# An attention and mixture-of-experts layer on one core: 38 of the 64 experts run in pairs as plain fp32 in the two column halves of TensorE

## The chip, the cores and the metric

The kernel runs on one core of a Trainium2 chip. The metric is the device time of one execution in microseconds (us); the times before are three runs, and one further execution was recorded by the hardware profiler. A core has the engines TensorE (PE, with its weight loads shown apart as PEld), VectorE (DVE), ScalarE (ACT), GpSimd (POOL) and SyncE (SP, which here only issues transfers), and 16 DMA engines that move data between HBM and the core's memory. SBUF is the on-chip memory of 128 partitions, PSUM the accumulators that TensorE writes.

## The reference

One transformer layer on 512 tokens of 1024 numbers: two attention branches, a layer norm, and a mixture of experts with a second layer norm. The change touches the mixture of experts alone:

```python
scores = jax.nn.sigmoid((hf @ w_router).astype(jnp.float32))      # 512 tokens x 64 experts
...
_, top_idx = lax.top_k(jnp.where(emask, biased, -jnp.inf), TOP_K)  # 8 experts for each token
top_w = top_s / jnp.sum(top_s, -1, keepdims=True) * ROUTED_SCALE
...
def step(acc, inp):                                                # one expert e, its tokens t
    t, w, e = inp
    xb = x_pad[t]
    hb = jax.nn.silu(xb @ w1_e[e]) * (xb @ w3_e[e])                # 1024 -> 256
    return acc.at[t].add((hb @ w2_e[e]) * w[:, None]), None        # 256 -> 1024
...
shared = (jax.nn.silu(hf @ ws1) * (hf @ ws3)) @ ws2                # every token
return (routed + shared).reshape(b, s, d)                         # ffn
...
return layer_norm(ALPHA * h + ffn, ln2_g, ln2_b)
```

There are 512 x 8 = 4096 rows of work, 64 for a mean expert. Each expert has 3 MB of fp32 weights, 192 MB in all.

## The kernel before

The attention part runs until about 480 us and is left as it is but for one line of stores. What follows is the expert stage.

**Tiles.** A tile is a list of up to 128 token rows. `tiles` has 35 of them: the first four experts alone (fixed, so that work can start before the experts are sorted), two large experts alone, and 29 pairs of a large with a small expert. The experts were sorted by their number of tokens (`order`). In a pair the list holds the union of both experts' tokens, both experts are applied to all its rows, and each row has a weight for each expert, zero where it wasn't routed there. From the routing of the reference's own inputs the 35 lists hold 3905 rows.

**What one expert costs.** Its weights come as three loads of 1 MB (`expert_load`, L820, issued by SP: two for the first products, one for the last), each into one page of SBUF. There are 16 pages; 5 hold shared weights and the transposed tokens until the shared expert is done, then 5 are taken by tiles called `dum`, so that 9 or 10 are left for expert weights. ACT and DVE split each half page into a high and a low part (`split`, L196 and L197; `LOOK` = 2 pieces ahead), and every product is made of three matmuls in fp32r (`mm3`, L302 to L304). An expert has six steps of 12 half products: four steps of the first product (`p_` 0 to 3) and two of the last (`p_` 4 and 5, which run among the next expert's steps), 36 matmuls of 512 columns.

**Rows in and out.** For each tile POOL issues a gather, an indirect transfer that brings the listed rows (4 KB each) from `hD` in HBM into the tile's partitions, one row for each partition (`gather_rows`, L1178), and a scatter that adds the tile's results to the rows of `accD` in HBM (`finish`, L1219). Empty slots are out of bounds and move nothing. PE transposes the gathered rows (L1190).

**What accD holds.** At first ALPHA times the tokens (`ya` in `h_rows`, made by ACT and stored from its queue). The shared expert's four blocks are added by POOL's accumulating transfers (`shared_out`, L1250), whose work is strewn between the expert steps. After the last scatter `accD` is loaded in four blocks `z` and normalised (L1475 to L1491).

**Order.** The expert stage stands in a `manual_schedule`: every engine, DVE and SP included, executes in the order in which the loop over `steps` writes the instructions. A load waits on SP until its page is free, which for a page of weights is when DVE has split its second half.

Of the kernel before, what the change touches and what calls it, by code (L numbers as in the profile page):

```python
# [19 lines left out]
S, D = 512, 1024  # L20
NE = 64
N_STAT = 4
N_SOLO = 2
N_TILE = N_STAT + N_SOLO + (NE - N_STAT - N_SOLO) // 2
# [14 lines left out]
for _k, _w in (("cb", 128), ("dn", 256), ("dp", 256), ("ut", 128), ("inv", 8), ("tok", 8),  # L39
               ("ident", 128), ("iota1", 128), ("lt", 64), ("lte", 64), ("rq", 128), ("stat", 3)):  # L40
    _C[_k] = (_n, _n + _w)
    _n += _w
# [4 lines left out]
def const_pack():  # L47
# [20 lines left out]
    rq[N_STAT:N_STAT + N_SOLO] = np.arange(N_SOLO)  # L68
    npair = (64 - N_STAT - N_SOLO) // 2
    m = np.arange(npair)  # L70
    rq[N_STAT + N_SOLO::2] = N_SOLO + m
    rq[N_STAT + N_SOLO + 1::2] = N_SOLO + 2 * npair - 1 - m
# [6 lines left out]
    tok[:, :, 1] = 128.0 * np.arange(4)[None] - 512.0  # L79
# [51 lines left out]
def hybrid_layer_kernel(tc, xT, xn, pos, w_idx, w_blk, w_uk, w_uv, w_ab, w_o, w_r, w_s13, w_s2, w_e, ln, b_gate,  # L131
# [514 lines left out]
    aoT = [None, None]  # L646

# [175 lines left out]


# [105 lines left out]
    pos1 = cpool.tile([128, 4, N_TILE], F32, name="pos1")  # L930
    pos0 = cpool.tile([128, 4, N_STAT], F32, name="pos0")
    hD = dpool.tile([S, D], F32, name="hD")
    accD = dpool.tile([S, D], F32, name="accD")
# [81 lines left out]
    def h_rows(c):  # L1015
# [18 lines left out]
        ya = t4([D], name="ya")  # L1034
        if YG:
            G.tensor_scalar(ya, hz[c], ALPHA, None, op0=OP.mult)
        else:
            A.activation(ya, hz[c], AF.Copy, scale=ALPHA)
        nc.scalar.dma_start(accD[c * 128:(c + 1) * 128], ya)
# [14 lines left out]
    def one_hot(pos_, i):  # L1054
        oh = t2([4, 128], BF16, name="oh")
        V.tensor_tensor(oh, C("iota1").unsqueeze(1).broadcast_to([128, 4, 128]),
                        pos_[:, :, i].unsqueeze(2).broadcast_to([128, 4, 128]), op=OP.is_equal)
        return oh

    def slot_mm(oh, qs, tw_):  # L1060
# [5 lines left out]
        if tw_ is not None:  # L1066
            for c in range(4):
                mm(pl[:, 2:2 + 3 * len(qs)], lhsT=oh[:, c],
                   rhs=tw_[:, c, qs[0]:qs[0] + len(qs)].rearrange("p q a -> p (q a)"), start=(c == 0), stop=(c == 3))
        return pl  # L1070

    def slot_rows(pl):

        lo_ = small([1], "li", bufs=4)
        V.tensor_scalar(lo_, pl[:, 1:2], 512.0, None, op0=OP.add)
        ii = small([1], "ii", I32, bufs=8)
        V.tensor_tensor(ii, pl[:, 0:1], lo_, op=OP.add)
        return ii

    def slot_weights(pl, n):  # L1080
        wv = small([2], "wv", bufs=8)
        V.tensor_reduce(wv[:, :n], pl[:, 2:2 + 3 * n].rearrange("p (q a) -> p q a", a=3), axis=AX.X, op=OP.add)
        return wv

    def tile_list(oh, qs, tw_):
        pl = slot_mm(oh, qs, tw_)
        return [slot_rows(pl), slot_weights(pl, len(qs))]

    tiles = [[q] for q in range(N_STAT + N_SOLO)]
    tiles += [[q, q + 1] for q in range(N_STAT + N_SOLO, NE, 2)]  # L1090
# [7 lines left out]
    selt = cpool.tile([128, 4, N_TILE], BF16, name="selt")  # L1098

    def order():  # L1100
# [46 lines left out]

        q0 = N_STAT + N_SOLO
        V.tensor_copy(selt[:, :, :q0], selq[:, :, :q0])
        V.tensor_tensor(selt[:, :, q0:], selq[:, :, q0::2], selq[:, :, q0 + 1::2], op=OP.max)  # L1150
        yield
        places(pos1, selt, N_TILE)
# [4 lines left out]
    def spill():  # L1157
        q0 = N_STAT + N_SOLO
        pc = ps_o()
        for c in range(4):  # L1160
            mm(pc[0:1, 0:N_TILE], lhsT=ones_b[:, 0:1], rhs=selt[:, c], start=(c == 0), stop=(c == 3))
        nt = t2([3, N_TILE], name="nt")[0:1]
        for b in range(3):
            V.tensor_scalar(nt[:, b], pc[0:1, 0:N_TILE], 128.5 + 128.0 * b, None, op0=OP.is_gt)
        V.tensor_tensor(nt[:, 0], nt[:, 0], nt[:, 1], op=OP.add)
        V.tensor_tensor(nt[:, 0], nt[:, 0], nt[:, 2], op=OP.add)
        V.tensor_copy(nbi[:, 0:q0], nt[:, 0, 0:q0])
# [347 lines left out]
```

## Time and profile before

| what | value |
|---|---|
| median of three runs | 1146.54 us (1145.93 to 1146.61) |
| the profiled execution's own time | 1148.03 us |
| its span, first to last instruction | 1146.3 us |
| PE / DVE / ACT / POOL busy in the span | 94% / 77% / 61% / 20% |
| bytes moved by the DMA engines | 285.99 MB, mean 249 GB/s |
| mean granted clock of PE | 0.974 of 2.4 GHz |

Busy shares are averages over the span. The profile also lists who waited for whom, the chain of work that ended last, and the share of the 16 DMA engines that was busy in a stretch. That share sums the times of packets, which overlap a little, so it can pass 1. A plain fp32 matmul has two records in the trace, an fp32r one has one.

### The profile page before, as it was taken

How to read it: one execution, taken by the hardware profiler on the slowest of the kernel's cores; microseconds unless marked ns; L12 is line 12 of the kernel's file. 1: busy time of each engine (PE TensorE's matmuls, PEld its weight loads, DVE VectorE, ACT ScalarE, POOL GpSimd, SP SyncE). 2: the span in 40 equal slices, each digit the busy share in tenths (PEclk: the TensorE clock that was granted, in tenths of full speed). 3: DMA queues.
4: the chain of work that ended last, by engine and by line, in shares of the span. 5: the costliest groups of instructions: out<-in, count | busy, mean ns of one | idle time of the engine just before them, and what ended most of it. 6: DMA issues, size and time to landing. Idle time of an engine off the chain costs nothing.

```text
span 1146.3 us, 15930 instructions
## 1 busy us (share of the span) xinstructions
PE 1073.5 (94%) x5453; PEld 856.3 (75%) x5454; DVE 886.4 (77%) x1716; ACT 693.9 (61%) x1079; POOL 224.1 (20%) x138
## 2 busy tenths in 40 slices
PE   8999999999999997899999999999999999999970
PEld 7777988767778886477777888887878888777750
DVE  6588567863224976678878999999999999989966
ACT  5652454544532512157767888888888788777850
POOL 0323422121240003212211111111212111111110
PEclk9989999999999998899999999999999999999995
DMA  9322100203115563579999899999999999999943
GB/s 350 123 74 74 37 7 32 75 1 111 38 57 208 197 246 110 204 262 317 336 383 363 287 371 401 383 397 384 389 394 381 399 382 398 383 394 384 383 115 149
DMA packets 51157, 285.99 MB, mean 249 GB/s; under 512 B 8574, under 2 KB 8830, under 8 KB 22784
## 3 DMA queue, kind: packets, MB, share of 16 engines
q1 hardware_dynamic: 37392, 240.09, 53.3%
q0 software_dynamic: 11088, 37.24, 12.6%
q10 hardware_dynamic: 2592, 7.60, 1.9%
q8 instruction: 44, 0.72, 0.2%
q14 instruction: 41, 0.34, 0.1%
HBM read 262.86 MB, written 26.76 MB: 253 GB/s over the span
## 4 chain that ended last, share of the span: by engine, by line
PE 78%; DVE 12%; DMA 5%; ACT 3%; issue 2%; SPq 0%; ACTq 0%; POOLq 0%; DVEq 0%
PE pj L302 12%; PE pj L304 11%; PE pj L303 11%; PE ps_s L303 10%; PE ps_s L302 10%; PE ps_s L304 10%; DMA we<-in_w_e_dram 3%; PE ps_t L1190 3%; PE pj L1229 2%; DVE sp L197 1%; PE pj L1247 1%; PE ps_o L1207 1%; ACT aw L599 1%; DVE aw L669 1%; PE ps_o L678 1%
## 5 line engine op out<-in xcount | busy, mean ns | idle before, releaser
L197 DVE TENSOR_TENSOR sp<-we,sp 128x1024 fp32r<-128x1024 f32 x379 | 446.7, 1220 | 29.6 <-ACT sp L196 25.5
L196 ACT CAST sp<-we 128x1024 fp32r<-128x1024 f32 x384 | 381.8, 1051 | 12.5 <-DMA we<-in_w_e_dram 7.5
L302 PE MATMUL ps_s<-sp,xt 128*128 128x512 f32 x512 | 222.4, 434 | 0.0
L303 PE MATMUL ps_s<-sp,xt 128*128 128x512 f32 x512 | 203.7, 398 | 1.0 <-DVE sp L197 1.0
L304 PE MATMUL ps_s<-sp,xt 128*128 128x512 f32 x512 | 202.1, 395 | 0.0
L197 POOL TENSOR_TENSOR sp<-raw,sp 128x1024 fp32r<-128x1024 f32 x38 | 90.8, 2388 | 232.5 <-ACT sp L196 232.5
L1219 POOL DMA_INDIRECT accD<-y,ii x35 | 56.3, 1609 | 384.2 <-ACT si L1200 325.8
L303 PEld LDWEIGHTS ps_s<-sp,xt 128*128 128x128 f32 x512 | 96.7, 189 | 33.2 <-DVE sp L197 12.4
L302 PEld LDWEIGHTS ps_s<-sp,xt 128*128 128x128 f32 x512 | 96.5, 189 | 23.5 <-issue 4.3
L304 PEld LDWEIGHTS ps_s<-sp,xt 128*128 128x128 f32 x512 | 96.2, 188 | 20.4 <-issue 0.2
L302 PE MATMUL pj<-sp,at 128*128 128x512 f32 x256 | 100.6, 393 | 0.0
L304 PE MATMUL pj<-sp,at 128*128 128x512 f32 x256 | 100.1, 391 | 0.0
L303 PE MATMUL pj<-sp,at 128*128 128x512 f32 x256 | 99.7, 389 | 0.0
L302 PE MATMUL pj<-sp,xh 128*128 128x512 f32 (+1 forms) x224 | 94.5, 424 | 5.0 <-ACT sp L196 5.0
L303 PE MATMUL pj<-sp,xh 128*128 128x512 f32 (+1 forms) x224 | 87.2, 389 | 0.1
L304 PE MATMUL pj<-sp,xl 128*128 128x512 f32 (+1 forms) x224 | 86.9, 388 | 0.0
L1178 POOL DMA_INDIRECT xg<-hD,ii x35 | 49.3, 1407 | 139.3 <-PE ps_t L1190 119.6
L196 ACT CAST sp<-raw 128x1024 fp32r<-128x1024 f32 (+2 forms) x45 | 45.2, 1004 | 50.2 <-PE pj L304 38.1
L302 PEld LDWEIGHTS pj<-sp,xh 128*128 128x128 f32 x224 | 55.3, 248 | 12.4 <-ACT sp L196 4.7
L196 ACT CAST xt<-ps_t 128x512 fp32r<-128x512 f32 x70 | 41.1, 587 | 38.6 <-PE ps_t L1190 36.4
L1218 ACT COPY y<-pj 128x512 f32<-128x512 f32 x69 | 40.1, 587 | 33.8 <-PE pj L304 31.0
L303 PEld LDWEIGHTS pj<-sp,xh 128*128 128x128 f32 x224 | 56.0, 250 | 3.8 <-DVE sp L197 0.5
(365 smaller groups left out, 1833.6 us busy)
## 6 DMA issues: line engine op xcount, KB each, us to landing
we<-in_w_e_dram SPq DMA_DIRECT2D x189, 1024.0 KB
raw<-in_w_blk_dram SPq DMA_DIRECT2D x20, 1024.0 KB
raw<-in_w_o_dram SPq DMA_DIRECT2D x4, 1024.0 KB
rab<-in_w_ab_dram SPq DMA_DIRECT2D x4, 768.0 KB
s<-in_w_s_dram SPq DMA_DIRECT2D x3, 1024.0 KB
we<-in_w_e_dram POOLq DMA_DIRECT2D x3, 1024.0 KB, 11.2
xr<-in_xT_dram SPq DMA_DIRECT2D x8, 256.0 KB
hD<-h ACTq DMA_DIRECT2D x4, 512.0 KB
```

The source lines that it names most:

```text
L196: A.copy(hi, raw)
L197: (eng or V).tensor_tensor(lo, raw, hi, op=OP.subtract)
L302: mm(o_, lhsT=ah, rhs=bh, start=start, stop=False)
L303: mm(o_, lhsT=ah, rhs=bl, start=False, stop=False)
L304: mm(o_, lhsT=al, rhs=bh, start=False, stop=stop)
L599: A.activation(aw[:, hh, :n], aw[:, hh, :n], AF.Exp, scale=0.125, bias=nms[hh], accum_out=den[hh])
L669: V.tensor_scalar(L, L, rd, None, op0=OP.mult)
L1178: G.indirect_dma_start(out=xg, out_offset=None, in_=hD[:, :], in_offset=bass.IndirectOffsetOnAxis(ap=ii[:, 0:1], axis=0), bounds_check=S - ...
L1190: T.transpose(pt[:, k * 128:(k + 1) * 128], xg[:, kk_ * 128:(kk_ + 1) * 128], ident)
L1218: A.copy(y[:, n * 512:(n + 1) * 512], py[n])
L1219: G.indirect_dma_start(out=accD[:, :], out_offset=bass.IndirectOffsetOnAxis(ap=ii[:, 0:1], axis=0), in_=y, in_offset=None, compute_op=OP.a ...
L1229: mm(p_, lhsT=hT[c // 2][:, c % 2, kt], rhs=s13[kt // 4][:, kt % 4], start=(kt == 0), stop=(kt == 7))
```

## The change

- **Tiles.** 45 instead of 35: the four fixed experts and 22 more alone (the 22 largest of the sorted ones), and 19 pairs of the 38 smaller ones. Pairs and single experts alternate, three single ones stand last (`tile_plan`). By the reference's routing the largest expert in a pair has 64 tokens.
- **Pairs.** The first expert has slots 0 to 63, the second slots 64 to 127, each its own list (`one_hot`, `slot_mm`). The lists hold 4096 rows. The weights are used as they come, without `split`: one plain fp32 matmul for each half, with 64 stationary columns, into its own half of the PSUM partitions. `xt` and `at` of a pair are one fp32 copy. The page of a pair's weights becomes free when PE has used it, not when DVE has split it.
- **Sums.** `accD` has 1024 rows; the second expert of a pair adds to the upper 512 (`jj`), since a token may be in both halves of one transfer. Both halves are set to zero early: POOL clears a tile, ACT issues eight stores in the attention part. `ya` and its stores go. The shared expert's rows are stored to `shD` from ACT's queue instead of being added by POOL.
- **The end.** At the first step of the third tile from the end SP issues eight loads of `hD` and `shD` (4 MB) into the four `z` pages; at the first step of the last tile but one DVE adds them (L1469), and SP loads the upper half of `accD`; at the first step of the last tile DVE adds that (L1473). After the last scatter the lower half is loaded and added (L1521), then normalised as before.
- **Pages.** The `dum` tiles go, so 14 pages serve weights once the shared expert is done. Single experts keep three split pieces in hand (`HOLD`), taken past a pair.

```diff
+N_SOLO = 22
+N_PAIR = (NE - N_STAT - N_SOLO) // 2
+N_END = 3
+def tile_plan():
+    tiles, q, s = [[i] for i in range(N_STAT)], N_STAT, 0
+    for m in range(N_PAIR):
+        tiles.append([q, q + 1])
+        q += 2
+        while s * N_PAIR < (m + 1) * (N_SOLO - N_END):
+            tiles.append([q])
+            q, s = q + 1, s + 1
+    return tiles + [[q + j] for j in range(N_END)]
...
+    accD = dpool.tile([2 * S, D], F32, name="accD")
+    shD = dpool.tile([S, D], F32, name="shD")
...
+        zero = t4([D], name="zero")
+        G.memset(zero, 0.0)
+        for a_ in range(0, 2 * S, 128):
+            nc.scalar.dma_start(accD[a_:a_ + 128], zero)
...
-        ya = t4([D], name="ya")
...
-            A.activation(ya, hz[c], AF.Copy, scale=ALPHA)
-        nc.scalar.dma_start(accD[c * 128:(c + 1) * 128], ya)
...
-        G.dma_start(accD[c * 128:(c + 1) * 128], y, accum_op=OP.add)
+        nc.scalar.dma_start(shD[c * 128:(c + 1) * 128], y)
...
-            while len(pieces) <= LOOK and len(pieces) < len(steps) - n:
-                split_next()
-            hi, lo = pieces.pop((q, p_))
+            while len(pieces) < HOLD:
+                if not split_next():
+                    break
+            if not pair:
+                hi, lo = pieces.pop((qs[0], p_))
...
+                    if pair:
+                        for q, rs_ in zip(qs, HALF):
+                            w1_ = wts[q][k // 4].rearrange("p (k n) -> p k n", k=4)
+                            mm(phs[i][rs_], lhsT=xts[i][:, k, rs_], rhs=w1_[:, k % 4], start=(k == 0), stop=(k == 7))
...
+            if i == NTL - N_END and p_ == 0:
+                for c in range(4):
+                    zs.append(page([2, D], name="z"))
+                    nc.sync.dma_start(zs[c][:, 0], hD[c * 128:(c + 1) * 128])
+                    nc.sync.dma_start(zs[c][:, 1], shD[c * 128:(c + 1) * 128])
+            if i == NTL - 2 and p_ == 0:
+                for c in range(4):
+                    V.scalar_tensor_tensor(zs[c][:, 0], zs[c][:, 0], ALPHA, zs[c][:, 1], op0=OP.mult, op1=OP.add)
+                    nc.sync.dma_start(zs[c][:, 1], accD[S + c * 128:S + (c + 1) * 128])
+            if i == NTL - 1 and p_ == 0:
+                for c in range(4):
+                    V.tensor_tensor(zs[c][:, 0], zs[c][:, 0], zs[c][:, 1], op=OP.add)
```

DVE at the end of the expert stage, before the change: `sp` is the low part of a split piece of weights, `si` and `at` are an expert's activation and its transposed low part, `y` is a result copied out of PSUM.

```order
L1201 SCALAR_TENSOR_TENSOR si<-si,wv,ps_s 128x256
L197 TENSOR_TENSOR sp<-we,sp 128x1024 x2
L197 TENSOR_TENSOR at<-ps_o,at 128x256
L197 TENSOR_TENSOR sp<-we,sp 128x1024 x4
L1201 SCALAR_TENSOR_TENSOR si<-si,wv,ps_s 128x256
L197 TENSOR_TENSOR sp<-we,sp 128x1024 x2
L197 TENSOR_TENSOR at<-ps_o,at 128x256
L197 TENSOR_TENSOR sp<-we,sp 128x1024 x3
L1201 SCALAR_TENSOR_TENSOR si<-si,wv,ps_s 128x256
L197 TENSOR_TENSOR at<-ps_o,at 128x256
L197 TENSOR_TENSOR sp<-we,sp 128x1024
L1216 COPY y<-pj 128x512
```

The same engine near the end, after the change (L217 is the old L197, L1228 the old L1201; `xt` is a low part of transposed rows):

```order
L217 TENSOR_TENSOR sp<-we,sp 128x1024
L1469 SCALAR_TENSOR_TENSOR z<-z 128x1024 x4
L217 TENSOR_TENSOR sp<-we,sp 128x1024
L217 TENSOR_TENSOR at<-ps_o,at 128x256
L217 TENSOR_TENSOR xt<-ps_t,xt 128x512
L217 TENSOR_TENSOR sp<-we,sp 128x1024 x2
L217 TENSOR_TENSOR xt<-ps_t,xt 128x512
L217 TENSOR_TENSOR sp<-we,sp 128x1024 x2
L1228 SCALAR_TENSOR_TENSOR si<-si,wv,ps_s 128x256
L217 TENSOR_TENSOR sp<-we,sp 128x1024
L1473 TENSOR_TENSOR z<-z 128x1024 x4
L217 TENSOR_TENSOR sp<-we,sp 128x1024
```

Four additions that read loaded `z` tiles (L1469) now stand on DVE ahead of the last eleven splits (four more follow the rows shown), and four more (L1473) ahead of the last five.

SP at the end of the expert stage, after the change, from the last expert's last load on (L841 is the old L820). Before it, the last load of weights was followed by nothing until the stage was over.

```order
L841 DMA we<-in_w_e_dram 128x2048
L1465 DMA z<-hD 128x1024
L1466 DMA z<-shD 128x1024
L1465 DMA z<-hD 128x1024
L1466 DMA z<-shD 128x1024
L1465 DMA z<-hD 128x1024
L1466 DMA z<-shD 128x1024
L1465 DMA z<-hD 128x1024
L1466 DMA z<-shD 128x1024
L1470 DMA z<-accD 128x1024 x4
```

The eight loads of `z` are issued behind the last load of weights, on the same queue.

## Rows read from the trace of the kernel before

**Rows 1.** Stretches of the expert stage: us, busy time by engine, clock, DMA share, GB/s

```profile
700.00:750.00 50.00, 50.00 (x254) 40.14 (x252) 47.92 (x62) 40.45 (x55) 7.67 (x5) 1.00 1.02 387
...
1000.00:1050.00 50.00, 49.24 (x249) 38.73 (x248) 45.94 (x61) 39.44 (x53) 7.48 (x5) 1.00 1.02 395
```

**Rows 2.** Waits, 700 to 1080 us: ACT's, then SP's queue

```profile
ACT sp L196 <- DMA we<-in_w_e_dram: 7.5, 6, 2.4
...
SPq L820 <- DVE sp L197: 275.8, 106, 4.5
```

**Rows 3.** The chain that ended last, 985 to 1147 us: start, length, what

```profile
1002.17 20.18 DMA we<-in_w_e_dram
...
1040.19 19.42 DMA we<-in_w_e_dram
```

**Rows 4.** Line L820, the weight loads: issues from 1002.1 to 1040.1 us; after 493 us

```profile
L820 SPq DMA_DIRECT2D we<-in_w_e_dram x12: 332/333/338, 1002.2 to 1035.5; - x12
...
L820 SPq DMA_DIRECT2D we<-in_w_e_dram x180: 332/333/722, 493.3 to 1080.7; - x180
```

**Rows 5.** Two stretches with one kind of transfer: weights alone; the first gather alone

```profile
394.00:400.00 6.00, 6.00 (x29) 4.95 (x28) 6.00 (x10) 2.06 (x5) 0.00 (x0) 1.00 1.00 421
...
481.20:482.20 1.00, 1.00 (x9) 0.29 (x8) 0.00 (x0) 0.00 (x0) 1.00 (x2) 0.50 0.53 86
```

**Rows 6.** Gathers after 495 us; gathers 700 to 1090 us; all scatters

```profile
L1178 POOL DMA_INDIRECT xg<-hD,ii x32: 1015/1500/1819, 497.2 to 1050.4; - x32
...
L1178 POOL DMA_INDIRECT xg<-hD,ii x20: 1287/1501/1512, 700.9 to 1050.4; - x20
...
L1219 POOL DMA_INDIRECT accD<-y,ii x35: 1564/1581/2209, 512.9 to 1112.7; - x35
```

**Rows 7.** Chain: plain fp32 matmuls, full width and halves, fp32r matmul, transposes

```profile
266.21 1.02 PE ps_o L678 x16
...
458.89 6.87 PE pj L1229 x16
...
1083.12 0.44 PE ps_t L1190 x4
...
1107.02 0.23 PE pj L302
```

**Rows 8.** Groups on DVE by form, 700 to 1080 us: busy, mean ns, idle before

```profile
L197 DVE TENSOR_TENSOR sp<-we,sp 128x1024 fp32r<-128x1024 f32 x250 | 294.5, 1220 | 16.3 <-ACT sp L196 13.9
...
L197 DVE TENSOR_TENSOR xt<-ps_t,xt 128x512 fp32r<-128x512 f32 x41 | 28.0, 683 | 0.0
...
L1201 DVE SCALAR_TENSOR_TENSOR si<-si,wv,ps_s 128x256 f32<-128x256 f32 x41 | 19.6, 478 | 3.5 <-ACT si L1200 3.3
L197 DVE TENSOR_TENSOR at<-ps_o,at 128x256 fp32r<-128x256 f32 x41 | 17.1, 418 | 0.0
```

**Rows 9.** Chain from the end of PE's work on; then a DVE group after 1111 us

```profile
1111.22 0.70 DVE y L1216
...
1112.73 6.17 DMA accD<-y,ii
1119.02 3.30 DMA z<-accD
1122.35 1.30 DVE bs L1480 x2
...
L1482 DVE SCALAR_TENSOR_TENSOR z<-z,mv,ln 128x1024 f32<-128x1024 f32 x4 | 5.1, 1282 | 0.1
```

**Rows 10.** Tile ya: its copies on ACT and its stores on ACT's queue

```profile
L1038 ACT ACTIVATE ya<-h x4: 1048/1063/1070, 413.5 to 468.4; 128x1024 f32<-128x1024 f32 x4
L1039 ACTq DMA_DIRECT2D accD<-ya x4: 326/333/333, 414.8 to 470.2; - x4
```

**Rows 11.** PE's clock around an idle stretch

```profile
440.00:445.00 5.00, 1.08 (x5) 0.56 (x3) 5.00 (x7) 0.81 (x1) 5.00 (x3) 0.98 0.41 121
445.00:450.00 5.00, 0.95 (x5) 0.98 (x6) 5.00 (x15) 0.00 (x0) 1.55 (x1) 0.50 0.27 110
```

More of the change, by code (lines that the diff above doesn't have):

```diff
@@ L67, in const_pack @@
     rq[:N_STAT] = 1000 + np.arange(N_STAT)
[L68 to L72, printed above, removed]
+    solo = [t[0] for t in TILES[N_STAT:] if len(t) == 1]
+    rq[solo] = np.arange(N_SOLO)
+    for m, t in enumerate([t for t in TILES if len(t) == 2]):
+        rq[t] = N_SOLO + m, N_SOLO + 2 * N_PAIR - 1 - m
+    cap = np.full(64, 64.0)
+    cap[solo + list(range(N_STAT))] = 128.0
+    put("cap", cap[None])
+    put("half", np.where(p >= 64, 512.0, 0.0))
     put("rq", np.where((np.arange(128) // 64)[None, :] == (np.arange(128) // 64)[:, None], np.tile(rq, 2)[None], -7.0))
@@ L1086, in tile_list @@
         pl = slot_mm(oh, qs, tw_)
[L1087 to L1090 removed]
+        return [slot_rows(pl, len(qs) == 2), slot_weights(pl)]
+    tiles = TILES
     lists = {}
@@ L1366, in hybrid_layer_kernel @@
     LG = (1,)
-    dummies, ln2 = [], []
+    ln2, zs = [], []
     phs, sis, ats, pys = {}, {}, {}, {}
+    lq = [tl[-1] for tl in tiles]
     with tc.manual_schedule():
-        for n, (q, p_) in enumerate(steps):
-            i = tile_of[q]
-            first, last = q == tiles[i][0], q == tiles[i][-1]
+        for n, (i, p_) in enumerate(steps):
+            qs = tiles[i]
+            pair = len(qs) == 2
             if n in OST:
@@ L1406, in hybrid_layer_kernel @@
             else:
                 f = p_ - 4
-                if first and f == 0:
+                if f == 0:
                     pys[i] = [pj(), pj()]
                 for n_ in range(2):
-                    mm3(pys[i][n_], ats[q][:, 0, f], ats[q][:, 1, f], hi[:, n_], lo[:, n_], first and f == 0,
-                        last and f == 1)
-                if last and f == 1:
+                    if pair:
+                        for m, rs_ in enumerate(HALF):
+                            w2_ = wts[qs[m]][2].rearrange("p (f n) -> p f n", f=2)
+                            mm(pys[i][n_][rs_], lhsT=ats[i][:, f, rs_], rhs=w2_[:, f, n_ * 512:(n_ + 1) * 512],
+                               start=(f == 0), stop=(f == 1))
+                    else:
+                        mm3(pys[i][n_], ats[i][:, 0, f], ats[i][:, 1, f], hi[:, n_], lo[:, n_], f == 0, f == 1)
@@ L1421, in hybrid_layer_kernel @@
[L1421 removed]
+            if p_ == 4 and i + 2 < NTL:
+                xpose(i + 2, 1)
+            if n == 2:
                 xpose(1, 1)
[L1423 to L1428 removed]
+            if i == NTL - N_END and p_ == 0:
[3 more added lines that the diff above has]
+                    nc.sync.dma_start(zs[c][:, 1], shD[c * 128:(c + 1) * 128])
@@ new lines, in hybrid_layer_kernel @@
+            if i == NTL - 2 and p_ == 0:
[5 more added lines that the diff above has]
+                    V.tensor_tensor(zs[c][:, 0], zs[c][:, 0], zs[c][:, 1], op=OP.add)
+            if i == NTL - 1 and p_ == 3:
+                sis[i] = act_si(phs.pop(i), lists[i][1])
+                ats[i] = act_t(sis.pop(i), not pair)
```

201 lines of the change are left out of this document (96 added, 105 removed).

## The prediction, made before the changed kernel ran

> **What bounds the kernel now.** I read the stretches of the expert stage first [rows 1]. PE is busy 50.00 of 50 us from 700 to 750 us, at full clock, and the 16 DMA engines have a busy share of 1.02. Two resources are full, so the question is which one the other waits for. The list of waits [rows 2] says that it changes. Over 380 us ACT waits only 7.5 us for a weight load to land, and SP spends 275.8 us waiting for DVE to free a page: for most of the stage PE's pace sets when loads may start. But the chain of work that ended last [rows 3] goes twice through a load that took about 20 us from its issue to its landing, at 1002 and at 1040 us. A load alone costs far less: in the stretch where nothing but weights moved, 1.00 share gave 421 GB/s [rows 5], so 1.049 MB take 2.49 us. A load that takes 20 us stands in a queue. From about 1000 us DMA sets the pace.
>
> That gives the price of a tile on DMA. The first of those loads landed at 1002.17 + 20.18 = 1022.35 us, the second at 1040.19 + 19.42 = 1059.61 us, 37.26 us later, and 12 loads were issued in between [rows 4], two pairs of experts. Twelve loads by 2.49 are 29.9 us. The other 7.4 us are two gathers and two scatters: **3.68 us for a tile's rows in and out**. PE's own pace in the stretch before is nearly the same, 18.39 us for a pair (19 intervals between 20 gathers, 700.9 to 1050.4 us) [rows 6] against 18.63 here. Before this change PE and DMA are in balance within 1.5%.
>
> Rows are not shared evenly by the DMA engines. While the first gather ran alone, the share of busy DMA engines was 0.53 [rows 5], and that tile has 67 rows in its 128 slots, 0.52. So an engine serves slots that are its own, and stands idle when they are empty; the engines of the first slots have eight rows in every tile. A load of weights is complete when the last of its 16 engines is, so the fullest engine sets the pace. The Trainium skill, page "DMA: Bandwidth & Descriptors", section "The descriptor swizzle", says which slots are whose (four from one half of 64 and four from its other half, for each engine); no row here shows that.
>
> **The change part by part.** *PE, the pairs.* Now a pair is 72 fp32r matmuls of 0.23 us [rows 7], 16.6 us. After it, it is 24 plain ones. The shared expert's eight plain fp32 matmuls of 512 columns took 6.87 us, 0.86 each; eight matmuls in column halves with 128 columns took 1.02 us, where a quarter of 0.86 each would be 1.72 [rows 7], so the halves overlap. 24 x 0.86 x 1.02/1.72 = 12.2 us. With transposes (2 x 0.44) and lists, about 0.6, a pair is near 13.7 us and a single expert (36 x 0.23 = 8.3) near 9.6: 23.3 us of PE for three experts against 1.5 x 18.39 = 27.6 us. This gain of 4.3 us is only had if weights arrive as fast.
>
> *DMA, the tiles.* They don't. Three experts need nine loads, 22.4 us, and now two tiles instead of one and a half. On the engines that serve the first slots each tile still costs 3.68 us, so three experts take 29.8 us of DMA, more than the 27.9 (1.5 x 18.63) of the DMA-bound stretch before, and more than PE's 23.3. PE will wait. ACT and DVE lose the splits of 38 experts, which frees engines that were not the limit.
>
> The sum runs from the first load of the sorted experts, 493.3 us [rows 4], to the last landing. Before: 180 loads and one of constants, 181 x 2.49 = 450.7; 32 gathers [rows 6] and 33 scatters, 32.5 x 3.68 = 119.6; four accumulating stores, bounded by a plain store (0.52 MB at 421 GB/s, 1.25) and a whole tile (3.68), taken as 2.4 since each is like a scatter, 9.6: 579.9 us. The last landing is near 1099 (1059.6 + 14 x 2.49 + about 4.6 for two scatters), so of 605.7 us some 26 were slack. After: the same 450.7; 42.5 tiles x 3.68 = 156.4; four plain stores 5.0: 612.1 us, already more than the whole stretch before. Slack does not vanish: until the first pair starts, the four fixed experts free pages at PE's pace as now, and a pair holds its pages until PE has used them, with 10 pages at hand. I take 20 us (10 to 27). The last landing is then 493.3 + 632.1 = 1125.4, **+26.4 us**. The bounds of the tile price on the fullest engine are 3.4 and 3.9, 12 us either way.
>
> *The end.* The eight loads of `z`, 4.2 MB, are queued behind the last weights and take 10.0 us at 421 GB/s. In DVE's written order the four additions that wait for them stand ahead of eleven splits. So DVE stops, and PE with it after at most three steps in hand, until 11.3 us after the last landing (10.0 + 1.28 for the last addition, as L1482 [rows 9]). Then DVE has 11 splits by 1.22, three `at` by 0.42, two `xt` by 0.68, two `si` by 0.48 [rows 8] and the four additions of L1473 by about 1.25: 22 us, of which some 0.5 overlap. PE's last step, 6 x 0.23 = 1.4, follows: PE ends 34.2 us after the last landing. Before it ended at 1111.2 [rows 9], 12.2 after. **+22.0 us**, between 12 (part of the splits is done by then) and 24.
>
> *The tail.* After the last scatter DVE has four more additions, 5 us, in a stretch where it has small gaps: **+4.0** (0 to 5).
>
> *Early.* Eight stores on ACT's queue cost ACT 8 x 0.33 us ahead of softmax work, and ACT waits for POOL's clearing; `ya`, 4 x 1.06 + 4 x 0.33, goes [rows 10]. On POOL the clearing delays splits behind it by about 1 us. Taken as 0 (-4 to +4). The slightly larger list work is a few tenths of a us for each tile beside an idle PE.
>
> Sum, against the profiled execution's own 1148.0: 1148.0 + 26.4 + 22.0 + 4.0 = 1200.4; the median is 1.5 lower, so **1199 us**.
>
> *PE's clock.* After 5 us with PE busy 1.08, the granted clock was 0.50, the lower level [rows 11]. PE will idle some 6 us in each three experts; if half speed for the next 10 us costs it 5 us, 28.3 us are still under 29.8. So nothing is added for it.
>
> **The rivals.** *A, rows spread evenly.* Were a tile's DMA price by its number of rows (3905/35 = 111.6 now, 4096/45 = 91 after), it would be 3.00 us, the last landing 1096.5, -2.5, and the time 1148 - 2.5 + 22 + 4 - 1.5 = 1170. The 0.53 speaks against.
>
> *B, the additions don't hold DVE.* If the `z` loads land before DVE gets there, the 22 go: 1177. That needs weights that are well ahead of PE at the end; by the sum they are not.
>
> *C, faster: rows cost DMA only their bytes.* The Trainium skill, "DMA: Bandwidth & Descriptors", section "Anatomy of one DMA", fits a transfer from GpSimd as a fixed 2 us plus its bytes at 436 GB/s. As a mechanism of this kernel: 91 rows in and out, 0.745 MB at 421 GB/s, are 1.77 us a tile; the last landing would be 493.3 + 450.7 + 75.2 + 25 = 1044, -55, and the time 1118. The price today speaks against: 111.6 rows would be 2.17 us by bytes, and 3.68 was measured. C decides from a price of 2.45 us a tile down, where the sum equals 1146.5.
>
> *D, the halves don't overlap, or a list overflows.* A pair would be 24 x 0.86 = 20.6 us, three experts 31.5 against 29.8, 19 times: +32, 1231. [rows 7] speaks against. And if a 65th token reached the largest paired expert, the loop after the stage would run for it, tens of us.
>
> **How the numbers follow.** Forecast 0.62, A 0.10, B 0.16, A and B together 0.02 (1148, no change), C 0.05, D 0.05. The forecast's own bounds (slack, tile price, end) give 1180 to 1214; A and B pull the low end to 1166: 1166 to 1214 leaves out C, D and A with B and the tails. Faster by over 0.2% is C, 0.05; within 0.2%, about what a measurement of this kernel can tell from no change, 0.02; slower 0.93.
>
> **What would show it.** In the profile after: PE busy about three quarters between 700 and 1050 us with DMA's share still near 1; ACT and PE waiting for weight loads by tens of us in total, SP hardly for DVE; gathers 14 to 15 us apart on average (29.8 for two); the last weights near 1125; then a stop of DVE of ten us or more in L1469, and PE ending over 30 us after the last landing. Single experts' matmuls stay at 0.23 us, halves near 0.5 for each fp32 matmul. It is wrong if gathers come under 13.5 us apart, which is A or C, or if DVE doesn't wait in L1469, which is B.

## The result: 1212.5 us, slower by 5.8%, and the profile after

| | before | after |
|---|---|---|
| median of the runs | 1146.26 us | 1212.45 us |
| ratio, 95% interval | | 1.0578 (1.0559 to 1.0596) |
| profiled execution, span | 1146.3 | 1209.2 |
| mean granted clock of PE | 0.974 | 0.930 |

The predicted 1199 us was 13 short; the range of 1166 to 1214 holds the time, close to its upper end. One run of a later kernel, the one with everything, came at a lower granted clock and was 3% longer than its others (1184.35 us at 0.832), and is left out of its median.

First the stretches of the expert stage. The columns are those of [rows 1]: the stretch, its length, the busy time of PE, PE's weight loads, DVE, ACT and POOL, then the clock, DMA's share and GB/s.

```profile
700.00:750.00 50.00, 43.51 (x231) 23.78 (x231) 20.32 (x35) 19.87 (x30) 8.23 (x6) 0.97 1.00 366
1000.00:1050.00 50.00, 45.53 (x230) 24.76 (x228) 20.95 (x37) 19.87 (x30) 8.11 (x6) 0.91 0.97 357
700.00:1050.00 350.00, 292.81 (x1463) 156.26 (x1463) 139.04 (x235) 135.53 (x210) 63.36 (x46) 0.91 0.99 366
```

Where [rows 1] has PE busy for 50.00 of 50 us beside a share of 1.02, PE now has gaps, 293 of 350 us busy, and DMA's share is 0.99 for 1.02 while it moves less, 366 GB/s for 387. The list of waits from 700 to 1080 us (engine and line, what it waited for, us in total, times, longest), rows of ACT, PE and SP, answers [rows 2]:

```profile
ACT sp L216 <- DMA we<-in_w_e_dram: 101.5, 12, 9.1
...
PE ps_o L1235 <- DVE si L1228: 57.1, 12, 5.4
...
SPq L841 <- DMA we<-in_w_e_dram: 142.2, 81, 2.9
SPq L841 <- PE ps_s L1437: 88.1, 15, 7.6
...
SPq L841 <- DVE sp L217: 16.3, 13, 2.1
```

ACT's wait for weights went from 7.5 to 101.5 us, SP's wait for DVE to be done with a split from 275.8 to 16.3: the weights set the pace. SP's largest wait is now for loads already issued to land, in 81 short pieces; it also waits 88.1 us for PE to free a pair's page, while loads issued earlier keep DMA's share at 0.99. PE has no row for weights: nearly all of its waiting, 57.1 us, is for `si`, an instruction of DVE that stands behind splits (a later experiment takes this up). The pace itself is in the group of gathers after 600 us (count, duration least/median/most in ns, first and last start):

```profile
L1200 POOL DMA_INDIRECT xg<-hD,ii x32: 1042/1066/2080, 601.5 to 1069.9; - x32
```

31 intervals in 468.4 us are 15.11 us each, 30.2 for the two tiles of three experts (predicted 29.8). The chain of work that ended last (start, length, what) shows the same, with PE between two loads, and then its end:

```profile
975.72 20.95 DMA we<-in_w_e_dram
996.79 27.20 DMA we<-in_w_e_dram
...
1028.48 3.61 PE ps_s L1437 x8
...
1034.79 1.89 PE ps_s L1437 x8
1036.68 20.16 DMA we<-in_w_e_dram
1056.96 27.77 DMA we<-in_w_e_dram
...
1096.74 26.59 DMA we<-in_w_e_dram
1123.34 12.88 DMA z<-shD
```

Loads of 20 to 28 us follow one another, where the chain of the kernel before has its first one in the stage at 1002 us [rows 3]. A step of a pair (L1437: four fp32 matmuls of 512 columns, two in each half, recorded as eight) takes 1.89 us at full clock, 0.47 each, but 3.61 in the step behind a wait, where the granted clock was 0.50. The last weights land at 1123.33 (1096.74 + 26.59). Behind them the chain waits 12.88 us for `z`. What that does to the engines, in the timeline of the end (start, length, engine, line, operation, tiles, in brackets the idle time before and who ended it): DVE's first and last L1469, then the next instruction of PE and of ACT that had waited long.

```profile
1126.27 1.23 DVE L1469 SCALAR_TENSOR_TENSOR z<-z 128x1024 f32<-128x1024 f32 x1 [2.91 <-DMA z<-shD]
...
1136.31 1.23 DVE L1469 SCALAR_TENSOR_TENSOR z<-z 128x1024 f32<-128x1024 f32 x1 [1.30 <-DMA z<-shD]
...
1138.73 0.79 PE L323 MATMUL pj<-sp,at 128*128 128x512 f32 x1 [12.38 <-DVE sp L217]
...
1142.12 0.59 ACT L216 CAST xt<-ps_t 128x512 fp32r<-128x512 f32 x1 [14.88 <-PE ps_t L1212]
```

DVE goes through four additions as their loads land, until 1137.54. PE stands for 12.38 us for the split behind them, ACT for 14.88 for PE's transposes, and what is queued on ACT stands too. Something like it happens once more behind the second four additions (L1473, 1148.05 to 1152.67), one row each of PE, ACT and DVE:

```profile
1153.86 0.79 PE L323 MATMUL pj<-sp,at 128*128 128x512 f32 x1 [4.00 <-DVE sp L217]
...
1158.96 0.38 ACT L1227 ACTIVATE si<-ps_s 128x256 f32<-128x256 f32 x1 [7.72 <-PE ps_s L324]
...
1159.38 0.48 DVE L1228 SCALAR_TENSOR_TENSOR si<-si,wv,ps_s 128x256 f32<-128x256 f32 x1 [1.83 <-ACT si L1227]
```

PE stands 4.00 us for a split. From 1153.86 to 1158.90 its granted clock is then 0.50, and eleven matmuls take 5.04 us, one about every 0.43 us where [rows 7] has 0.23. ACT waits for them, and DVE for ACT. The next rows are POOL's, where a scatter can't start until the one before it has landed, and SP's first load of the sums:

```profile
1146.12 1.58 POOL L1254 DMA_INDIRECT accD<-y,ii  x1 [23.20 <-ACT si L1227]
1163.29 1.56 POOL L1254 DMA_INDIRECT accD<-y,ii  x1 [15.58 <-ACT y L1252]
1170.80 1.55 POOL L1254 DMA_INDIRECT accD<-y,ii  x1 [5.95 <-DMA accD<-y,ii]
...
1177.45 1.75 SPq L1519 DMA_DIRECT2D z<-accD  x4
```

In [rows 9] the last scatter starts 1.5 us after PE's last matmul (1112.73, 1111.2). Here PE's last matmul ends at 1164.5 and the last scatter starts 6.3 later, since the scatter before it was itself issued only at 1163.29. Then 38.4 us to the end of the span, 33.6 before.

The sum of what was added: last landing 24.2 (1123.3 against about 1099.1, which is the prediction's estimate; DMA's share before is 0.08 from 1098 to 1099 us and 0.00 in the next one), PE's end behind it 29.0 (41.2 against 12.2), the last scatter behind PE 4.8, the tail 4.8: 62.8 us, the difference of the spans is 62.9.

### The profile page after: what moved, and what is told of

Its sections match the earlier page's. It is cut to its first block, busy times and chain, and to the rows that moved or that the text cites. A ratio compares the mean times of both kernels' runs of the same rounds, so it can differ in the third digit from the quotient of the medians.

```text
span 1209.2 us, 14859 instructions
## 1 busy us (share of the span) xinstructions
PE 1024.1 (85%) x5195; PEld 685.5 (57%) x5196; DVE 632.4 (52%) x1482; ACT 483.3 (40%) x849; POOL 242.1 (20%) x150
## 4 chain that ended last, share of the span: by engine, by line
PE 42%; DMA 40%; DVE 12%; issue 3%; ACT 3%; SPq 0%; ACTq 0%; POOLq 0%; DVEq 0%
DMA we<-in_w_e_dram 36%; PE pj L322 8%; PE pj L323 7%; PE pj L324 7%; PE ps_s L1437 5%; DMA accD<-y,ii 2%; PE ps_t L1212 2%; PE ps_s L322 1%; PE ps_s L323 1%; PE ps_s L324 1%; PE pj L1264 1%; DMA z<-shD 1%; ACT aw L619 1%; DVE aw L690 1%; ACT y L1252 1%
## 5 line engine op out<-in xcount | busy, mean ns | idle before, releaser
L217 DVE TENSOR_TENSOR sp<-we,sp 128x1024 fp32r<-128x1024 f32 x151 | 180.4, 1222 | 186.5 <-ACT sp L216 186.5
L216 ACT CAST sp<-we 128x1024 fp32r<-128x1024 f32 x156 | 158.1, 1051 | 147.3 <-DMA we<-in_w_e_dram 141.7
L1437 PE MATMUL ps_s<-we,xtn 128*64 128x512 f32 x608 | 162.7, 672 | 0.0
L217 POOL TENSOR_TENSOR sp<-raw,sp 128x1024 fp32r<-128x1024 f32 x38 | 90.8, 2390 | 225.2 <-ACT sp L216 225.2
L322 PE MATMUL ps_s<-sp,xt 128*128 128x512 f32 x208 | 95.5, 459 | 0.0
L1437 PEld LDWEIGHTS ps_s<-we,xtn 128*64 128x64 f32 x608 | 44.0, 152 | 85.1 <-issue 81.1
L217 DVE TENSOR_TENSOR xt<-ps_t,xt 128x512 fp32r<-128x512 f32 x52 | 36.0, 691 | 97.7 <-ACT xt L216 97.7
L1254 POOL DMA_INDIRECT accD<-y,jj x19 | 30.2, 1591 | 274.9 <-DVE sp L217 166.2
L324 PE MATMUL ps_s<-sp,xt 128*128 128x512 f32 x208 | 82.7, 398 | 0.0
L323 PE MATMUL ps_s<-sp,xt 128*128 128x512 f32 x208 | 82.3, 396 | 0.0
L1448 PE MATMUL pj<-we,atn 128*64 128x512 f32 x304 | 73.6, 605 | 0.0
L1212 PE MATMUL ps_t<-c_all,xg 128*128 128x128 f32 x360 | 63.6, 306 | 10.6 <-DMA xg<-hD,ii 10.5
L1252 ACT COPY y<-pj 128x512 f32<-128x512 f32 x89 | 50.0, 585 | 41.2 <-PE pj L324 33.5
L1212 PEld LDWEIGHTS ps_t<-c_all,xg 128*128 128x128 f32 x360 | 47.9, 157 | 32.9 <-ACT sp L216 11.4
```

Source lines behind the costliest of these rows:

```text
L216: A.copy(hi, raw)
L217: (eng or V).tensor_tensor(lo, raw, hi, op=OP.subtract)
L322: mm(o_, lhsT=ah, rhs=bh, start=start, stop=False)
L323: mm(o_, lhsT=ah, rhs=bl, start=False, stop=False)
L324: mm(o_, lhsT=al, rhs=bh, start=False, stop=stop)
L1212: T.transpose(pt[:, k * 128:(k + 1) * 128], xg[:, kk_ * 128:(kk_ + 1) * 128], ident)
```

## The experiments

All are compared with the changed kernel, 1212.45 us, or with the run named; each diff is cut to its core.

### Is it the fullest DMA engine?

The prediction rests on 3.68 us for a tile's rows, set by the engine that serves the first slots. So the rows are laid into other slots, and every other pair swaps its halves. Nothing else is changed but four small buffers at the end, which become two to make room.

```diff
-    put("iota1", f + 1.0 + 0.0 * p)
+    r128, r64 = np.arange(128), np.arange(64)
+    slot = 64 * (r128 % 16 // 8) + 4 * (r128 % 8) + (r128 // 16 & 3) + 32 * (r128 // 64)
+    hslot = 4 * (r64 % 8) + (r64 // 8 & 3) + 32 * (r64 // 32)
+    put("iota1", 1.0 + np.argsort(slot)[None])
+    put("iotap", 1.0 + np.argsort(hslot)[None])
...
-        rq[t] = N_SOLO + m, N_SOLO + 2 * N_PAIR - 1 - m
+        rq[t[::1 - 2 * (m % 2)]] = N_SOLO + m, N_SOLO + 2 * N_PAIR - 1 - m
...
-                        C("iota1")[:, :128 // m].unsqueeze(1).unsqueeze(1).broadcast_to(sh),
+                        C("iota1" if m == 1 else "iotap").unsqueeze(1).unsqueeze(1).broadcast_to(sh),
```

`slot` gives neighbouring ranks of an expert's tokens to different engines. It follows the Trainium skill, "DMA: Bandwidth & Descriptors", "The descriptor swizzle": of a 1 MiB transfer to 128 partitions engine 0 writes 0 to 3 and 32 to 35, engine 1 the next four of both, and engines 8 to 15 the upper half likewise.

> The changed kernel with the rows of each tile laid into its 128 slots so that the 16 DMA engines get nearly equal numbers of them (every other pair of experts also changes halves). Theory, the fullest engine sets the pace: a tile cost 3.9 us with eight rows on that engine, 0.49 us a row. By the routing of the inputs its rows fall from 360 to about 276 in the 45 tiles, so the last weights land some 41 us earlier (near 1083 instead of 1123), a pair of gathers comes 13.5 to 14.5 us apart instead of 15.2, and the time is near 1172 (1165 to 1180). Rival, the price of a tile goes by its number of rows or is a fixed price for each indirect transfer: nothing moves, 1212 within 3 us. Rival, PE sets the pace (it was 83% busy): a gain of a few us at most.

Measured: 1171.67 us, 40.8 less. The stretch from 700 to 1050 us of this kernel, in the columns above:

```profile
700.00:1050.00 350.00, 302.12 (x1553) 160.18 (x1551) 147.79 (x248) 142.94 (x222) 69.43 (x50) 0.96 1.02 394
```

DMA is as full, but moves 394 GB/s. Its group of gathers after 600 us:

```profile
L1204 POOL DMA_INDIRECT xg<-hD,ii x34: 1032/1046/1552, 611.3 to 1078.6; - x34
```

A gather comes every 14.16 us: 28.3 for two tiles, 1.9 less. With nine loads at 2.49 a tile costs 2.96 us instead of 3.90, for 6.16 rows on the fullest engine instead of 8 (277 and 360 rows over 45 tiles). The number of rows is the same in both, so a price by rows or by transfers (rivals A and C) is out, and PE's pace too. The last weights land at 1086.0 (1063.99 + 22.02 in its chain), 37.3 us earlier where about 41 were expected; the rest came in the end, which the expectation did not count. The profile doesn't show which engine moved a row. But by that rule of the Trainium skill ("DMA: Bandwidth & Descriptors", "The descriptor swizzle") the slots were laid and the gain was forecast: this run agrees with it.

### What is the price of a row made of?

```diff
-                             in_=y, in_offset=None, compute_op=OP.add, bounds_check=n - 1, oob_is_err=False)
+                             in_=y, in_offset=None, bounds_check=n - 1, oob_is_err=False)
```

> The changed kernel with the scatters writing their rows instead of adding them (the sum over experts is left out, so the output is another). Theory, rows on the fullest engine set the pace and an added row costs it a read and a write: a gathered row and a written row would cost about the same, so a tile falls from 3.9 us to about 2.6, the last landing by 50 us or so, until PE's own pace (25 us in three experts against 22.4 + 5.2 of DMA) is near: time about 1155 to 1170. Rival, an indirect transfer has a fixed price whatever it does with its rows: 1212 within 5 us.

Measured: 1161.78 us in one run, 50.7 less.

```profile
L1200 POOL DMA_INDIRECT xg<-hD,ii x35: 1017/1202/1783, 600.9 to 1071.0; - x35
```

34 intervals of 13.83 us, 27.7 for two tiles: 2.62 us a tile. Eight rows in and out cost 0.49 us each when they are added, 0.33 when they are written, so by this run the adding is a third of the price.

### Is the end held by the additions?

```diff
-            if i == NTL - 2 and p_ == 0:
+            if n == len(steps) - 1:
                 for c in range(4):
                     V.scalar_tensor_tensor(zs[c][:, 0], zs[c][:, 0], ALPHA, zs[c][:, 1], op0=OP.mult, op1=OP.add)
                     nc.sync.dma_start(zs[c][:, 1], accD[S + c * 128:S + (c + 1) * 128])
-            if i == NTL - 1 and p_ == 0:
                 for c in range(4):
```

> The changed kernel with the eight additions on DVE that wait for z, the shared rows and the pairs' rows written behind DVE's last copy of y instead of ahead of the last splits; the loads stay where they are. Theory, these additions hold DVE and through it PE at the end: the last weights still land near 1123, PE ends 14 to 17 us after them instead of 41, the last scatter no longer waits for the one before it, and the tail grows by 0 to 5 us: the time falls by 24 to 32 us to about 1184 (1180 to 1189). Rival, the end is held by the transfers of z themselves or by the splits that are left: 1212 within 5 us.

Measured: 1193.56 us, 18.9 less, not 24 to 32. Nothing was moved but eight additions on DVE and SP's loads of the pairs' sums, which follow them, so the additions held 18.9 us; that much of the theory stands. Two things did not come. PE's last matmul ends at 1146.0, 18.5 earlier, but still some 22 us behind the last weights (issued last at 1099.5, with 24 us to land as for most loads here). And the last scatter still waits, by POOL's timeline:

```profile
1144.81 1.56 POOL L1254 DMA_INDIRECT accD<-y,ii  x1 [9.13 <-ACT y L1252]
1152.82 1.55 POOL L1254 DMA_INDIRECT accD<-y,ii  x1 [6.45 <-DMA accD<-y,ii]
```

It starts 6.8 us after PE's end, as late as with the additions.

### Do the two gains add?

The two diffs above in one kernel.

> Both edits, the spread rows and the additions behind the last copy of y. Theory: the two terms are apart in time, so their gains add: 1212 - 41 - 28 = 1143 (1136 to 1152), about the kernel before. If the end only hides what the spread rows gain, or the other way round, the gain is less than the sum of the two by ten us or more.

Measured: 1156.93 us, 55.5 less where the single gains sum to 59.7. They add but for four us; of the 14 us above the expected 1143, nine are the additions' smaller gain. The kernel is still 0.9% slower than before the change (ratio 1.0093, 1.0076 to 1.0110).

### Why does PE end so long after the last weights?

First guess: four single experts in a row stand at the end (the three of `N_END` and one that the loop puts behind the last pair), and their work is left when the weights are there. They are dealt out evenly instead; this and the next run have the additions last.

```diff
-        while s * N_PAIR < (m + 1) * (N_SOLO - N_END):
+        while s * N_PAIR < (m + 1) * N_SOLO:
...
-    return tiles + [[q + j] for j in range(N_END)]
+    return tiles
```

> The kernel with the additions last, and besides with the single experts dealt out evenly among all pairs, so that one single expert stands at the end instead of four in a row. In the trace with the additions last, PE is not idle for more than 1.1 us at a time from 1116 us on and takes 10.3 us for each of the last three tiles; it ends some 24 us after the last weights (near 1122). Theory, the row of single experts at the end is work of PE, ACT and DVE that is still to do when the weights are all there: with one single expert last, PE ends 12 to 16 us after the last landing and the time falls by 8 to 12 us, from 1193.6 to about 1183 (1179 to 1187). Rival, the end is set by the scatters that wait for one another: 1193 within 4 us.

Measured: 1197.75 us, 4.2 more than with the additions last. The theory fell. The trace shows another cause. In the timeline of the last pair, two rows of DVE and one of PE:

```profile
1122.21 1.23 DVE L217 TENSOR_TENSOR sp<-we,sp 128x1024 fp32r<-128x1024 f32 x1 [9.98 <-ACT sp L216]
1123.47 0.48 DVE L1228 SCALAR_TENSOR_TENSOR si<-si,wv,ps_s 128x256 f32<-128x256 f32 x1
...
1124.00 0.69 PE L1235 MATMUL ps_o<-c_all,si 128*128 128x128 f32 x2 [5.26 <-DVE si L1228]
```

DVE waits 9.98 us in a split (for ACT's half of it, which waits for weights), the `si` of the tile before stands behind it, and PE stands 5.26 us for that `si`. The split is a piece of the *next* single expert. The loop keeps three pieces in hand, and a pair needs none, so the piece is asked for a whole pair, six loads, early. It happens again and again, by PE's largest row in this kernel's list of waits from 700 to 1100 us:

```profile
PE ps_o L1235 <- DVE si L1228: 59.1, 11, 7.6
```

So the next kernel splits a piece only three steps ahead of its use:

```diff
+    at_step = {(tiles[i][0], p_): n for n, (i, p_) in enumerate(steps)}
...
             while len(pieces) < HOLD:
-                if not split_next():
+                if cut and at_step[cut[-1]] > n + HOLD or not split_next():
```

> The kernel of pairs to the end (1198) with one rule more for the order on DVE and ACT: a piece of a single expert's weights is split at most three steps ahead of PE's use. So far the rule was three pieces in hand: the first piece of the next single expert is then split before the si of the tile in hand, a whole pair (six loads) early. Theory: DVE waits in that split for weights that come behind the pair's, the si behind it waits with it, and PE with the si (5.2, 5.3 and 4.3 us at a time in that trace); this is why PE ended 22 us or more behind the last weights whatever stood at the end. With the rule PE ends 10 to 15 us behind them and the time is 8 to 14 us shorter, 1187 (1183 to 1190). Rival, these waits are only the DMA's pace seen at another place: the same time within 3 us.

Measured: 1189.41 us, 8.3 less. In the same list of this kernel the waits for `si` are gone, and PE waits for the pair's own weights instead. All its waits there sum to 55.2 us, from 70.6:

```profile
PE ps_s L1438 <- DMA we<-in_w_e_dram: 43.3, 12, 4.6
```

PE's last matmul starts at 1139.86, 8.1 us earlier than without the rule (1147.93). From 600 us on the gathers keep their pace, 14.9 us apart in both kernels. So the hold was a cost of its own and not DMA's pace seen elsewhere.

### Pairs without the new sums

The change has two halves, pairs and sums. This kernel has the pairs and the sums of before; it has besides the spread rows, the single experts dealt out and the two small edits of the next diff.

```diff
-        for a_ in range(0, 2 * S, 128):
-            nc.scalar.dma_start(accD[a_:a_ + 128], zero)
...
+        A.activation(ya, hz[c], AF.Copy, scale=ALPHA)
+        nc.scalar.dma_start(accD[c * 128:(c + 1) * 128], ya)
...
-        n = S if ii[0] is ii[1] else 2 * S
-        G.indirect_dma_start(out=accD[0:n, :], out_offset=bass.IndirectOffsetOnAxis(ap=ii[1][:, 0:1], axis=0),
-                             in_=y, in_offset=None, compute_op=OP.add, bounds_check=n - 1, oob_is_err=False)
+        for jj in ii[len(ii) - 2:] if ii[0] is not ii[1] else ii[:1]:
+            G.indirect_dma_start(out=accD[:, :], out_offset=bass.IndirectOffsetOnAxis(ap=jj[:, 0:1], axis=0),
+                                 in_=y, in_offset=None, compute_op=OP.add, bounds_check=S - 1, oob_is_err=False)
```

> The kernel with all of these, but with the sums as they were in the kernel before the change: accD set to ALPHA times h, shared rows added to it by DMA, no separate loads and additions of z at the end; the second experts of the pairs go into the same accD by a scatter of their own, which waits until the first one has landed. Takes the parts pairs and sums of the change apart. Theory: 8 loads of z (10 us of DMA behind the last weights) and four additions in the tail (5 us) fall away, the tail is again 33 to 35 us behind the last scatter: 1129 (1123 to 1136). Rival, POOL waits for the first scatter of each pair and holds up the gathers behind it, 8 to 10 us for each pair: then PE waits for rows and the time is 1140 or more.

Measured: 1290.97 us. The rival, and far worse than its 1140: in 350 us from 700 on POOL and PE wait like this:

```profile
POOL accD L1263 <- DMA accD<-y,j: 72.1, 9, 8.9
...
POOL accD L1263 <- DMA accD<-y,jj: 37.3, 4, 9.4
...
PE ps_t L1221 <- DMA xg<-hD,ii: 103.7, 10, 14.1
```

The second scatter of a pair waits for the first (`jj`), up to 9.4 us, the scatter after it for the second (`j`), the next gather is behind them on POOL, and PE waits 103.7 us for rows. So the second half of `accD`, and with it the additions at the end, is what lets a pair's rows go out in one scatter. In this order of POOL's work these sums can't simply be taken back.

### What is left of the gain?

Four more kernels try how far the pairs go. The first has everything: spread rows, additions last, single experts dealt out, every other tile's rows in the opposite order, and the last `act_t` (the transposes of an `si`) behind the last but one tile's final matmuls.

```diff
-                        C("iota1" if m == 1 else "iotap").unsqueeze(1).unsqueeze(1).broadcast_to(sh),
+                        C("iota1" if m == 1 else "iotap")[:, ::(1, -1)[mir[m - 1] // m % 2]].unsqueeze(1).unsqueeze(1).broadcast_to(sh),
...
                     finish(lists[i][0], pys.pop(i), n == len(steps) - 1)
+                    if i == NTL - 2:
+                        ats[i + 1] = act_t(sis.pop(i + 1), len(tiles[i + 1]) == 1)
```

> Everything so far in one kernel: rows spread, additions last, one single expert at the end, and two small things besides: every other tile fills the DMA engines in the opposite order (the rows of the fullest engine go from 277 to 259, by the routing), and the transposes of the last si stand behind the last but one tile's final matmuls, so that its scatter isn't late. From 1157 for spread rows and additions last: 18 rows by 0.49 are 9 us, of which I count 6 since PE is at 87%; the single experts 10; the scatter 4. Theory: 1137 (1131 to 1145), faster than the kernel before. If PE's pace takes over, the rows bring nothing and it is 1143 or more.

Measured: 1147.99 us (ratio to before 1.0029, 1.0013 to 1.0045), 8.9 less than spread rows and additions last, not 20. Ten of the 20 were for dealing out the single experts, which by itself had gained nothing in the run above; that these are what is missing here was not taken apart.

The same with late splits:

> The same rule in the kernel with everything (1149). Theory: the same 8 to 14 us less, 1138 (1134 to 1142), faster than the kernel before. Rival as in the run before: 1149 within 3 us; or the end is set by then by the scatters that wait for one another (the last was issued 6.9 us after the one before, and 4.7 us after PE's last matmul): 1145.

Measured: 1145.61 us (ratio 1.0002, 0.9992 to 1.0012). 2.4 less, not 8 to 14. In the kernel with everything PE's waits for a held `si` were 33.9 us (700 to 1100 us):

```profile
PE ps_o L1242 <- DVE si L1235: 33.9, 11, 7.0
```

With late splits they are gone, and all of PE's waits in that stretch fall from 53.5 to 35.4 us. This is more than was saved above, and yet PE's last matmul starts only 2.3 us earlier (1096.33 for 1098.62). So less waiting of PE in the stage is no time won here. The second rival, an end set by scatters that wait for one another, had 1145 and fits. The last three scatters stand in a row, here in the timeline of the kernel with late splits, where the trace puts the second down to ACT and the third to the landing of the second:

```profile
1083.89 1.58 POOL L1261 DMA_INDIRECT accD<-y,ii  x1 [15.64 <-ACT si L1234]
1093.95 1.56 POOL L1261 DMA_INDIRECT accD<-y,jj  x1 [8.47 <-ACT at L220]
1100.76 1.55 POOL L1261 DMA_INDIRECT accD<-y,ii  x1 [5.25 <-DMA accD<-y,jj]
```

Two kernels try to loosen that row. One does the last pair's second half two steps earlier:

```diff
-            if i > 0 and p_ in (2, 3):
+            if i > 0 and p_ in (2, 3) and i != NTL - 1:
                 steps.append((i - 1, 2 + p_))
+            if i == NTL - 1 and p_ == 1:
+                steps += [(i - 1, 4), (i - 1, 5)]
```

> As the run before, and the last pair's second half is done two steps earlier, before the last single expert's third and fourth steps, so that its scatter has landed and its sums are loaded when the last scatter is issued (the moved transposes of the last si go back to where they were). Theory: the last scatter waits no more (5 us) and lands in about 6.5 us as in the kernel before, instead of 9.9 with the loads of the pairs' sums beside it: 5 to 8 us below the run before, near 1131 (1127 to 1138). Rival, the pair's rows aren't ready earlier because its weights are not: the same as the run before within 2 us.

Measured: 1144.09 us (ratio 0.9986, 0.9972 to 1.0000), 1.5 less, not 14; within the rival's two us. The pair's rows were ready at 1092.9 (ACT's copy), but its scatter was issued at 1096.12, most likely for the single expert's scatter before it (issued at 1086.29), and the last waited for the pair's until 1103.02. The other puts two single experts last instead of one (`N_END = 1` in the plan of the change):

> The kernel with everything and late splits (1145.6) with two single experts at its end instead of one, so that the last pair's scatter comes some ten us earlier. In the two traces before, the last three scatters stand in a row, each waiting until the one before it has landed (7 to 10 us each beside the loads of z), and the last one was issued 4.7 us after PE's last matmul and took 8.4 us beside the loads of the pairs' sums. Theory, with late splits a single expert more at the end costs nothing (3 loads and its rows are 10 us of DMA, its work 10.3), the last scatter is issued 1.5 us after PE and lands in 6.5 us: 5 us less, 1140.5 (1137 to 1144), faster than the kernel before by half a per cent. Rival, the row of scatters only moves, or PE ends as much later: 1145 within 2 us.

Measured: 1145.25 us (ratio 0.9997, 0.9985 to 1.0009), no gain.

```profile
1097.12 1.56 POOL L1261 DMA_INDIRECT accD<-y,ii  x1 [8.03 <-ACT at L220]
1103.22 1.71 POOL L1261 DMA_INDIRECT accD<-y,ii  x1 [4.54 <-DMA accD<-y,ii]
```

The last but one scatter comes late now, by the trace behind ACT's `at`, and the last waits 4.54 us for it. The row of scatters only moved, as the rival had it; an order that frees it was not found.

### The kernel before, with its rows spread

```diff
-    put("iota1", f + 1.0 + 0.0 * p)
+    put("iota1", 1.0 + np.argsort(slot)[None])
```

> The kernel before the change with nothing but its rows spread over the DMA engines in the same way. Theory: PE set its pace until about 1000 us, DMA only the last 100 us; a tile there has some 112 rows of 128, so the fullest engine goes from 8 to 7 rows, 0.49 us a tile over some five or six tiles: 1 to 3 us, 1144.5 (1143 to 1146.3). Rival, DMA held it back through the whole stage: 35 tiles by 0.4, ten us or more.

Measured: 1143.54 us, ratio 0.9974 (0.9964 to 0.9985), 2.7 us less. The last scatter moves from 1112.73 [rows 9] to 1109.35. In its trace the gathers lead those of the kernel before by some 1.5 us from 600 to 1012 us, then by 2.9 at 1032 and by 3.2 at 1050. So DMA held the kernel before only at its end, as the prediction read from [rows 3]. This small edit has the lowest time of what was run, though not clear of the kernel with the last pair first (0.9986).

## Why the prediction was right, point by point, and where its terms were off

- **The bound.** PE and DMA in balance before, DMA alone in the stage after: shown. PE busy 84% (predicted three quarters) at a share of 0.99, SP's waits for DVE down from 292.7 us to 51.3 (all rows), two tiles 30.2 us against 29.8. One sign came in another form: PE did not wait for weight loads itself but for `si` behind splits that did, 57.1 us.
- **The price of a tile**, 3.68 us with bounds 3.4 and 3.9, measured 3.90 on this kernel, at the upper bound. That the fullest engine sets it, read from a share of 0.53 [rows 5] and 67 of 128 slots, is shown by the spread rows: 83 rows less on that engine by 0.49 are 40.5 us, the time fell by 40.8 and the last landing came 37.3 earlier. Rival A, 3.00 us a tile, is out.
- **The last landing**, 1125.4, measured 1123.3, 24.2 us later than before where 26.4 were predicted. That is luck in two terms: with tiles at 3.90 the same sum leaves 8.6 us of slack, not 20, which was a choice, and not the 10 to 27 of its bounds. The dearer tiles and the smaller slack offset each other.
- **PE's matmuls.** Halves took 0.47 us for each fp32 matmul (predicted near 0.5), so rival D is out. So is rival C: by bytes alone, at the 421 GB/s of [rows 5], a tile would cost 1.77 us; 3.90 was measured, 2.96 with its rows spread. The Trainium skill ("DMA: Bandwidth & Descriptors", "Anatomy of one DMA") lets the moving part of a transfer from GpSimd go by its bytes; these rows between queued loads cost more, and the measurement decides.
- **The clock.** Groups behind a wait ran at half speed, 3.61 us for 1.89, and PE with it was busy 25.3 of 30.2 us (293 of 350). In the stage it stayed under DMA's price, as predicted, and nothing had to be added. At the end there was no such cover, and the sum has no term for it.
- **The end**, +22.0, measured +29.0: right in its mechanism, DVE and then PE stopped in L1469 (so rival B is out), and mis-sized in two terms. The loads of `z` took 12.9 us, not 10.0; a scatter issued at 1121.33 and a gather issued at 1112.44 moved rows beside them, which is the likely reason and was not tested. DVE's list behind them took 25.5 us, not 21.5 (1137.5 to 1163.0), since it stopped for ACT, 4.9 us in all, which the sum had taken as idle. Of these, 1.6 are for casts that stood on ACT behind one that had waited for PE. The other 3.3 begin with the last `si`: PE had stopped a second time, for the split behind L1473, and came back at half clock, where eleven matmuls took 5.04 us instead of 2.5. The additions themselves hold PE's end by 18.5 of the 29, shown by moving them. Splits asked for a pair early cost 8.3 us, shown in the kernel with the single experts dealt out; how much of the 29 they are in the changed kernel was not run. The prediction did not see them: it had DVE's order at the end before it and did not ask what the rule of three pieces does in every pair.
- **The last scatter**, not in the sum at all: +4.8. The prediction took it as issued when PE is done, as in [rows 9], and so put its wait at nothing. Here the copies of the last but one `y` stand on ACT behind the last `at`, its scatter is issued with PE's last matmuls (1163.29), and the last one waits for it to land, 5.95 us.
- **The tail**, +4.0, measured 4.8.
- **Early**, 0: the first load of the sorted experts starts at 495.2 against 493.3 [rows 4], inside the bound of 4.

The terms predicted sum to 52.4 against 62.9 measured; 7 of the difference are in the end and 4.8 in the scatter. With 10 us more than the sum the time came 1.5 us inside the range.

## What to carry to other kernels

Fewer instructions on one engine buy nothing where a second resource is as full: weigh the change on both, and price a transfer on the DMA engine that gets most of it, not by its bytes. A partly filled list of rows should be dealt over the partitions so that all engines get their share. In a list written by hand, each instruction that waits for a late transfer, an addition or a split made too early, holds all that is queued behind it, and the engines that wait for those in turn.

## What the runs showed of the hardware

- A row of 4 KB gathered and added cost DMA's fullest engine 0.49 us, gathered and written 0.33 (3.90 and 2.62 us for eight; the second in one run).
- The price of a tile followed from the slots in which its rows were laid, also in an indirect transfer with empty slots: the same number of rows cost 3.90 or 2.96 us.
- A scatter that has to wait for the one before it waited up to 9.4 us while weights were loading (the kernel with one sum), where a tile's rows, in and out, cost some 3 us of DMA's time (2.96 with spread rows).
- After stops of 12.38 and 4.00 us near the end PE's granted clock was 0.50, the lower level of 1.2 GHz, from 1138.7 to 1142.3 and from 1153.86 to 1158.90 us; matmuls that take 0.23 us came every 0.43.
